# A two-layer hybrid diffusion trunk: modulation summed in halves of 512 features, rotated key and query rows put in place by GpSimd

## The chip, the cores and the metric

The kernel runs on one core of a Trainium2 chip. The metric is the device time of one execution in microseconds (us). A core has TensorE (PE, matmuls; its weight loads are listed as PEld), VectorE (DVE), ScalarE (ACT), GpSimd (POOL) and SyncE (SP), which issues nearly all transfers here. On-chip data lies in SBUF, results of PE in PSUM banks.

## What is computed

A trunk of two layers over 256 context and 256 latent tokens of 1024 features, in float32. Each layer modulates its normalised input by vectors made from a condition, runs three attention mixers on it, merges them by gates, and then runs a SwiGLU FFN. Cut to what matters:

```python
def adaln(cond, w, b):
    return jnp.split(jax.nn.silu(cond) @ w + b, 6, axis=-1)      # six kinds of 1024 features

for l in range(2):
    mx = adaln(c, w_ada[l], b_ada[l])                            # latent tokens
    mc = adaln(c_ctx, w_ada[l], b_ada[l])                        # context tokens
    hx = rms_norm(x, pre[l]) * (1 + mx[1]) + mx[0]               # hc alike, from ctx and mc
    kv = (rms_norm(ckv, kv_norm) @ w_ukv)                        # 8 heads: 64 of key, 64 of value
    q  = (rms_norm(cq, q_norm) @ w_uq)                           # 8 heads: 64 plain, 32 to be rotated
    qr, kr = rope_2d(q[..., 64:]), rope_2d(kr)                   # kr: one key of 32 for all heads
    scores = qn @ kn + qr @ kr                                   # 96 rows per head, then softmax
    ...                                                          # differential and windowed attention
    x = x + mx[2] * rms_norm(merge(o_a, o_b, o_c, gates), post[l])
    f = swiglu(rms_norm(x, ffn_pre[l]) * (1 + mx[4]) + mx[3])
    x = x + mx[5] * rms_norm(f, ffn_post[l])                     # context tokens alike in layer 0 only
```

Kinds 0, 1, 3 and 4 of the modulation scale and shift an input and are needed with features on partitions; kinds 2 and 5 (here called gates) multiply a sub-layer's output and are needed as rows that are the same on all partitions. The output is the latent stream after layer one.

## The kernel before

The token stream stands as four tiles of 128 tokens, two of context and two of latents; layer zero works on all four, layer one on the two latent tiles for queries and FFN. All weights come in blocks of up to 512 KB through SyncE into `raw` tiles (L166; three buffers) and are split into a high and a low part of a shorter float format: ACT casts the high part (L139, L142), DVE subtracts for the low one (L140, L143). A product is then three matmuls (`mm3`, L267 to L269: high by high, high by low, low by high).

PE and SyncE run what is issued to them in the order in which the program is written. For ACT, DVE and POOL a scheduler sets the order by priority, and code under `tc.high_priority()` goes ahead of what is ready at the same time.

`drive` (L241) writes that order: it runs the matmuls of the weight units one after another, counts their cost, and between them takes steps of an attention generator (`side`) and of a filler. The filler here is `ada_dve` (L341), the modulation's product. For each kind it goes through four quarters of 256 features. A quarter is two loads of 512 KB (`aw`, two buffers, L350); DVE multiplies each row by one element of the condition and accumulates, for the latent and the context condition apart (L401 the first piece, L403 the other seven of each): 16 pieces of 128x256 in all, or 8 where only one condition is needed. What is left is a sum over partitions, and that is `finish`, which is run half a quarter later: PE sums by matmuls with ones (L361), ACT copies the sums (L363), and for kinds 0, 1, 3 and 4 PE transposes them (L367) and DVE adds bias and weight (`mod_finish`). For a gate the sums go through DRAM: a row is written (L372), bias and norm weight are broadcast (L376, L377), the row is read back on all partitions (L380), and DVE adds and multiplies (L382, L383).

The filler serves layer zero's mixers (kinds 4, 3 and 2), layer zero's FFN (5 for layer zero; 1, 0, 4 and 3 for layer one), layer one's mixers (kind 2) and its FFN (kind 5): ten jobs of four quarters, 40 finishes, 24 with transposes, of which eight for one condition only (64 rows), and 16 for gates. In the FFN of layer zero PE meanwhile runs the gate and up projections; ACT applies the activation (L1271), DVE multiplies by the up part (L1272), and the product is split into `aT` by L139 and L140.

In the mixers `ukv` (L1025) makes keys and values of the latent attention for a group of four heads: two products for the keys, copied by ACT (L1033, L1034) into `kT` rows 0 to 63, four for the values, copied by DVE into `mv` (L1038), and four copies of the rotated shared key `krT` into rows 64 to 95 (L1040, DVE). `uq` (L1045) does the same for the queries: the rotated part goes through `rope` (L631: a shuffle and a multiply on DVE, a multiply and an add on POOL, L638 and L639) into a work tile, and four DVE copies put it into rows 64 to 95 of `qT` (L1061). The scores (L723), their maximum (L665), exponential (L669), scaling (L745, L747), combination of pairs (L805, L806), transposes (L675) and their copies (L678) are steps of the attention generator. L554 is the product for the first modulation vectors at the kernel's start, also with 32 columns of a condition and 256 columns of a weight.

## Time and profile before

| What | us |
|---|---|
| Median of three runs | 1523.82 |
| Lowest and highest of them | 1520.46 and 1524.37 |
| The profiled execution | 1522.53 |
| Its span in the trace | 1520.7 |
| PE busy in the span | 1457.6 |
| DVE busy in the span | 1022.9 |
| ACT busy in the span | 688.2 |
| POOL busy in the span | 154.6 |

PE is busy nearly all the time, so the profile is read from its gaps: first the table by stretches, which tells where they are, then the waits of PE, which tell what ended last in them, and then the timeline at the places named there. A wait in the lists of the other engines is of interest only where PE comes to wait behind it.

### The profile page before, as it was taken

How to read it: one execution, taken by the hardware profiler on the slowest of the kernel's cores; microseconds unless marked ns; L12 is line 12 of the kernel's file. 1: busy time of each engine (PE TensorE's matmuls, PEld its weight loads, DVE VectorE, ACT ScalarE, POOL GpSimd, SP SyncE). 2: the span in 40 equal slices, each digit the busy share in tenths (PEclk: the TensorE clock that was granted, in tenths of full speed). 3: DMA queues.
4: the chain of work that ended last, by engine and by line, in shares of the span. 5: the costliest groups of instructions: out<-in, count | busy, mean ns of one | idle time of the engine just before them, and what ended most of it. 6: DMA issues, size and time to landing. Idle time of an engine off the chain costs nothing. (4 is left out here: it accounts for less than half of the span.)

```text
span 1520.7 us, 23166 instructions
## 1 busy us (share of the span) xinstructions
PE 1457.6 (96%) x8827; PEld 1225.4 (81%) x8827; DVE 1022.9 (67%) x1987; ACT 688.2 (45%) x1293; POOL 154.6 (10%) x217
## 2 busy tenths in 40 slices
PE   7989999998999999999899999999999999999998
PEld 5867877776777879877676888877798899799986
DVE  4689768788884555778877314678667776666654
ACT  5566544444553354222222223666455564544443
POOL 1232100121100000000000000242102200100000
PEclk9999999999999999999999999999999999999999
DMA  9533222443333542665566225334345436567664
GB/s 290 154 108 98 66 88 85 110 111 111 98 97 101 172 144 73 184 182 171 180 206 198 95 97 170 108 80 139 94 116 142 132 100 195 180 209 218 207 213 166
DMA packets 254244, 216.25 MB, mean 142 GB/s; under 512 B 24427, under 2 KB 236085, under 8 KB 254133
## 3 DMA queue, kind: packets, MB, share of 16 engines
q1 hardware_dynamic: 252464, 209.98, 46.8%
q10 hardware_dynamic: 1668, 4.80, 0.8%
q8 instruction: 69, 1.13, 0.3%
q14 instruction: 43, 0.34, 0.1%
HBM read 209.48 MB, written 5.27 MB: 141 GB/s over the span
## 5 line engine op out<-in xcount | busy, mean ns | idle before, releaser
L267 PE MATMUL psg<-hT,hl 128*128 128x256 f32 (+1 forms) x1328 | 474.6, 357 | 0.0
L269 PE MATMUL psg<-hT,hl 128*128 128x256 f32 (+1 forms) x1328 | 449.4, 338 | 0.1
L268 PE MATMUL psg<-hT,hl 128*128 128x256 f32 (+1 forms) x1328 | 449.2, 338 | 0.3 <-DVE hT L460 0.3
L140 DVE TENSOR_TENSOR hl<-raw,hl 128x1024 fp32r<-128x1024 f32 (+2 forms) x243 | 291.1, 1199 | 207.2 <-ACT hl L139 206.4
L139 ACT CAST hl<-raw 128x1024 fp32r<-128x1024 f32 (+2 forms) x243 | 243.6, 1004 | 312.4 <-PE psg L269 176.7
L267 PEld LDWEIGHTS psg<-hT,hl 128*128 128x128 f32 x1328 | 252.9, 190 | 37.3 <-issue 13.9
L269 PEld LDWEIGHTS psg<-hT,hl 128*128 128x128 f32 x1328 | 252.4, 190 | 28.4 <-DVE hl L140 0.3
L268 PEld LDWEIGHTS psg<-hT,hl 128*128 128x128 f32 x1328 | 253.2, 191 | 24.6 <-issue 3.6
L403 DVE SCALAR_TENSOR_TENSOR acc<-aw,siluc,acc 128x256 f32<-128x256 f32 x448 | 200.2, 484 | 10.4 <-DMA aw<-in_w_ada 7.8
L477 POOL TENSOR_SCALAR smy<-ssy 128x1 f32<-128x1 f32 x12 | 4.1, 339 | 727.0 <-ACT work L298 727.0
L675 PE MATMUL psT<-ca,work 128*128 128x128 f32 x400 | 65.0, 277 | 10.4 <-DVE work L747 6.2
L669 ACT ACTIVATE work<-psS,nm 128x512 f32<-128x512 f32 (+1 forms) x96 | 59.1, 616 | 33.1 <-DVE nm L667 16.1
L267 PE MATMUL psg<-oT,hl 128*128 128x512 f32 (+1 forms) x192 | 69.5, 362 | 0.0
L675 PEld LDWEIGHTS psT<-ca,work 128*128 128x128 f32 x400 | 48.6, 142 | 22.6 <-issue 12.4
L665 DVE TENSOR_REDUCE nm<-psS 128x1 f32<-128x512 f32 (+1 forms) x96 | 57.1, 595 | 14.2 <-PE psS L723 8.9
L269 PE MATMUL psg<-oT,hl 128*128 128x512 f32 (+1 forms) x192 | 64.8, 338 | 0.2 <-DVE hl L140 0.2
L268 PE MATMUL psg<-oT,hl 128*128 128x512 f32 (+1 forms) x192 | 64.6, 337 | 0.0
L678 ACT COPY work<-psT 128x512 f32<-128x512 f32 (+1 forms) x72 | 36.8, 511 | 57.9 <-PE psT L675 56.5
L267 PE MATMUL psg<-hl,hT 128*128 128x256 f32 (+1 forms) x168 | 58.0, 345 | 1.9 <-ACT hT L139 1.9
L269 PE MATMUL psg<-hl,hT 128*128 128x256 f32 (+1 forms) x168 | 48.4, 288 | 0.6 <-DVE hT L140 0.6
L268 PE MATMUL psg<-hl,hT 128*128 128x256 f32 (+1 forms) x168 | 48.0, 286 | 0.0
L745 ACT ACTIVATE work<-work,rsd 128x512 f32<-128x512 f32 (+1 forms) x48 | 31.3, 652 | 36.2 <-DVE rsd L741 36.0
(324 smaller groups left out, 2578.5 us busy)
## 6 DMA issues: line engine op xcount, KB each, us to landing
raw<-in_w_gate_up SPq DMA_DIRECT2D x88, 512.0 KB
aw<-in_w_ada SPq DMA_DIRECT2D x80, 512.0 KB
raw<-in_w_in SPq DMA_DIRECT2D x78, 512.0 KB
raw<-in_w_down SPq DMA_DIRECT2D x44, 512.0 KB
aw<-in_w_ada SPq DMA_DIRECT2D x32, 256.0 KB
raw<-in_w_o SPq DMA_DIRECT2D x16, 512.0 KB
raw<-in_w_branch_a SPq DMA_DIRECT2D x8, 512.0 KB
raw<-in_w_in SPq DMA_DIRECT2D x16, 256.0 KB
```

The lines of the kernel that those rows point to most:

```text
L139: nc.scalar.copy(hi, src)
L140: nc.vector.tensor_tensor(lo, src, hi.bitcast(F32), ALU.subtract)
L267: nc.tensor.matmul(ps, lhsT=asl(a[0], k), rhs=bsl(b[0], k), start=st, stop=False)
L268: nc.tensor.matmul(ps, lhsT=asl(a[0], k), rhs=bsl(b[1], k), start=False, stop=False)
L269: nc.tensor.matmul(ps, lhsT=asl(a[1], k), rhs=bsl(b[0], k), start=False, stop=en)
L403: nc.vector.scalar_tensor_tensor(acc[:, s], w[:, k], sc, acc[:, s], ALU.mult, ALU.add)
L477: nc.gpsimd.tensor_scalar(sm, ss[:, 0:1], ss[:, 1:2], D * EPS, ALU.add, ALU.add)
L665: nc.vector.tensor_reduce(nm, ps[:, :nk], AX.X, ALU.max, negate=True)
L669: nc.scalar.activation(st["p"][:, :nk], ps[:, :nk], AF.Exp, bias=nm, accum_out=sm)
L675: nc.tensor.transpose(pt[:, k * P:(k + 1) * P], st["p"][:, k * P:(k + 1) * P], ident)
L678: nc.scalar.copy(st["pT"][:, :nk], pt[:, :nk])
L745: nc.scalar.activation(p, p, AF.Copy, scale=rs[:, j:j + 1])
```

## The change

Four things are changed. The modulation goes through halves of 512 features in place of quarters: four loads of two weight rows per partition instead of two loads of four, so 80 loads of 512 KB as before; accumulate pieces of 128x512, half as many; 20 finishes in place of 40, each with sums over 256 columns, one copy of 256 columns, two transposes in one PSUM bank, and for a gate rows of 512. The finish runs under high priority (`ahead_of`) after half of the next half's pieces, and it reports a higher cost to the filler's account. The filler of layer zero's mixers is started when 30 cost units of that stretch have passed, where before it was started ahead of it. And the copies of the rotated key into `kT` are made by POOL, issued at the start of `ukv`; in `uq` POOL adds the two rotated halves straight into the four head slices of `qT`, so that the work tile and DVE's four copies are gone.

```diff
@@ -228,6 +228,15 @@
                 return
             fill["acc"] -= v
 
+    def ahead_of(gen):
+
+        while True:
+            with tc.high_priority():
+                v = next(gen, None)
+            if v is None:
+                return
+            yield v
+
     def flush():
         if fill["D"] is not None:
             for _ in fill["D"]:
@@ -341,72 +350,78 @@
     def ada_dve(*jobs):
 
 
-        todo = [(l, kind, ns, q) for l, kind, ns in jobs for q in range(4)]
-
-        def raw(i, h):
-            l, kind, _, q = todo[i]
-            w = sp.tile([P, 4, 256], F32, tag="xt", bufs=2, name="aw")
-            c0 = kind * D + q * 256
-            nc.sync.dma_start(w, w_ada[l, h * 512:(h + 1) * 512, c0:c0 + 256].rearrange("(k p) n -> p k n", p=P))
+        H = D // 2
+        todo = [(l, kind, ns, hf) for l, kind, ns in jobs for hf in range(2)]
+
+        def raw(i, j):
+            l, kind, _, hf = todo[i]
+            w = sp.tile([P, 2, H], F32, tag="xt", bufs=2, name="aw")
+            c0 = kind * D + hf * H
+            nc.sync.dma_start(w, w_ada[l, j * 256:(j + 1) * 256, c0:c0 + H].rearrange("(k p) n -> p k n", p=P))
             return w
 
-        def finish(l, kind, ns, q, acc):
+        def finish(l, kind, ns, hf, acc):
             m = mods[l, kind]
             gate = kind in (2, 5)
             n = 64 * ns
             ps = bank("T")
-            for f in range(2):
+            for g in range(2):
                 for s in range(ns):
-                    j = 32 * (2 * s + f if gate else ns * f + s)
-                    nc.tensor.matmul(ps[j:j + 32, :P], lhsT=ones[:, :32], rhs=acc[:, s, f * P:(f + 1) * P], start=True, stop=True)
-            sums = work()[:, :P]
-            nc.scalar.copy(sums[:n], ps[:n, :P])
-            yield 0.8
+                    j = 32 * (2 * s + g if gate else ns * g + s)
+                    if gate:
+                        src = acc[:, s, g * 256:(g + 1) * 256]
+                    else:
+                        src = acc[:, s].rearrange("p (b g c) -> p b g c", b=2, g=2)[:, :, g]
+                    nc.tensor.matmul(ps[j:j + 32, :256], lhsT=ones[:, :32], rhs=src, start=True, stop=True)
+            sums = work()[:, :256]
+            nc.scalar.copy(sums[:n], ps[:n, :256])
+            yield 1.2
             if not gate:
                 ps = bank("T")
-                nc.tensor.transpose(ps[:, :n], sums[:n], ident[:n, :n])
-                mod_finish(l, kind, 2 * q, m, ps[:, :n].rearrange("p (f s z) -> p f s z", s=ns, z=32)[:, :, :, 0])
-                yield 0.2
+                for b in range(2):
+                    nc.tensor.transpose(ps[:, b * n:(b + 1) * n], sums[:n, b * P:(b + 1) * P], ident[:n, :n])
+                mod_finish(l, kind, 4 * hf, m, ps[:, :2 * n].rearrange("p (f s z) -> p f s z", s=ns, z=32)[:, :, :, 0])
+                yield 0.3
                 return
-            row = dp.tile([2 * ns, P], F32, name=f"row{l}_{kind}_{q}")
+            row = dp.tile([2 * ns, 256], F32, name=f"row{l}_{kind}_{hf}")
             nc.sync.dma_start(row, sums[0:n:32])
-            bw = work().rearrange("p (a b) -> p a b", a=2)
+            bw = [work(), work()]
             w = attn_post if kind == 2 else ffn_post
-            c0 = kind * D + q * 256
-            nc.sync.dma_start(bw[:, 0], b_ada[l:l + 1, c0:c0 + 256].to_broadcast([P, 256]))
-            nc.sync.dma_start(bw[:, 1], w[l:l + 1, q * 256:(q + 1) * 256].to_broadcast([P, 256]))
-            yield 1.0
-            mq = m[:, :ns, q * 256:(q + 1) * 256]
-            nc.sync.dma_start(mq, row.rearrange("(s f) p -> s (f p)", s=ns).rearrange("(o s) n -> o s n", o=1).to_broadcast([P, ns, 256]))
+            c0 = kind * D + hf * H
+            nc.sync.dma_start(bw[0], b_ada[l:l + 1, c0:c0 + H].to_broadcast([P, H]))
+            nc.sync.dma_start(bw[1], w[l:l + 1, hf * H:(hf + 1) * H].to_broadcast([P, H]))
+            yield 1.5
+            mq = m[:, :ns, hf * H:(hf + 1) * H]
+            nc.sync.dma_start(mq, row.rearrange("(s g) p -> s (g p)", s=ns).rearrange("(o s) n -> o s n", o=1).to_broadcast([P, ns, H]))
             for s in range(ns):
-                nc.vector.tensor_tensor(mq[:, s], mq[:, s], bw[:, 0], ALU.add)
-                nc.vector.scalar_tensor_tensor(mq[:, s], mq[:, s], 32.0, bw[:, 1], ALU.mult, ALU.mult)
-            yield 0.5 * ns
+                nc.vector.tensor_tensor(mq[:, s], mq[:, s], bw[0], ALU.add)
+                nc.vector.scalar_tensor_tensor(mq[:, s], mq[:, s], 32.0, bw[1], ALU.mult, ALU.mult)
+            yield 1.0 * ns
 
         nxt = raw(0, 0)
         pend = None
-        for i, (l, kind, ns, q) in enumerate(todo):
-            if q == 0:
+        for i, (l, kind, ns, hf) in enumerate(todo):
+            if hf == 0:
                 gate = kind in (2, 5)
                 mods[l, kind] = bp.tile([P, 2, D], F32, tag="gw", bufs=1, name="gw") if gate else mod_tile(kind)
-            acc = sp.tile([P, 2, 256], F32, tag="acc", bufs=2, name="acc")
-            for h in range(2):
+            acc = sp.tile([P, 2, H], F32, tag="acc", bufs=2, name="acc")
+            for j in range(4):
                 w = nxt
-                if h == 0 or i + 1 < len(todo):
-                    nxt = raw(i + h, 1 - h)
-                for k in range(4):
+                if j < 3 or i + 1 < len(todo):
+                    nxt = raw(i + j // 3, (j + 1) % 4)
+                for k in range(2):
                     for s in range(ns):
-                        sc = siluc[:, s, 4 * h + k:4 * h + k + 1]
-                        if h == 0 and k == 0:
+                        sc = siluc[:, s, 2 * j + k:2 * j + k + 1]
+                        if j == 0 and k == 0:
                             nc.vector.tensor_scalar(acc[:, s], w[:, k], sc, None, ALU.mult)
                         else:
                             nc.vector.scalar_tensor_tensor(acc[:, s], w[:, k], sc, acc[:, s], ALU.mult, ALU.add)
-                    yield 0.38 * ns
-                if h == 0 and pend is not None:
-                    yield from pend
-            pend = finish(l, kind, ns, q, acc)
+                    yield 0.76 * ns
+                if j == 1 and pend is not None:
+                    yield from ahead_of(pend)
+            pend = finish(l, kind, ns, hf, acc)
         yield 2.0
-        yield from pend
+        yield from ahead_of(pend)
 
 
     cur = {}
@@ -1027,6 +1042,8 @@
                 if g == 0:
                     env["mv"] = s8([P, 4, 512], F32, "mv")
                 kT = env["kT", g] = s8([P, 4, 512], F32, "kT")
+                for h in range(4):
+                    nc.gpsimd.tensor_copy(kT[64:96, h, :], env["krT"][64:96])
                 for h in range(0, 4, 2):
                     ps = bank()
                     yield from mm3(ps, parts, env["ckvT"], cols(h * 64, h * 64 + 128), full, range(2))
@@ -1036,8 +1053,6 @@
                     ps = bank()
                     yield from mm3(ps[:, :256], env["ckvT"], parts, tok(t), cols(256, 512), range(2))
                     nc.vector.tensor_copy(env["mv"][:, t, g * 256:(g + 1) * 256], ps[:, :256])
-                for h in range(4):
-                    nc.vector.tensor_copy(kT[64:96, h, :], env["krT"][64:96])
                 while put_off:
                     put_off.pop(0)()
             return f
@@ -1052,13 +1067,16 @@
                     nc.scalar.copy(qT[0:64, h + 1, TQ0:512], ps[64:128, :NQ])
                 ps = bank()
                 yield from mm3(ps[:, :NQ], parts, env["cqT"], cols(256, 384), cols(TQ0, 512), range(2))
-                r = work()
-                rope(r[:, :256], ps[:, NQ - 256:NQ], slice(0, P), c32, s32, SH8)
+                lat = ps[:, NQ - 256:NQ]
+                sh, t1 = (sp.tile([P, 256], F32, tag=tag, bufs=2, name=tag) for tag in ("rsh", "rt1"))
+                nc.vector.stream_shuffle(sh, lat, SH8)
+                nc.vector.tensor_tensor(t1, lat, c32, ALU.mult)
+                nc.gpsimd.tensor_tensor(sh, sh, s32, ALU.mult)
                 for h in range(4):
                     rows = slice(32 * h, 32 * h + 32)
                     if not last:
                         nc.scalar.copy(qT[64:96, h, 0:256], ps[rows, 0:256])
-                    nc.vector.tensor_copy(qT[64:96, h, 256:512], r[rows, :256])
+                    nc.gpsimd.tensor_tensor(qT[64:96, h, 256:512], t1[rows], sh[rows], ALU.add)
             return f
 
         for g in range(2):
@@ -1427,10 +1445,11 @@
                            lambda h, k: env["mv"][:, k, h * 64:(h + 1) * 64], False, lambda t: None)
         drive(1)
         if l == 0:
-            start_fill(ada_dve((0, 4, 2), (0, 3, 2), (0, 2, 2)), FR[0])
+            later = [(30.0, lambda: start_fill(ada_dve((0, 4, 2), (0, 3, 2), (0, 2, 2)), FR[0]))]
         else:
+            later = ()
             start_fill(ada_dve((1, 2, 1)), FR[2])
-        drive(count(("ukv", "uq", "dk", "dq", "dv")), attend(mla, PRM["LD"][0]), PRM["R1"][l])
+        drive(count(("ukv", "uq", "dk", "dq", "dv")), attend(mla, PRM["LD"][0]), PRM["R1"][l], later)
         drive(count(("gate", "branch", "s")) - 24, attend(diff_steps(l, env), PRM["LD"][1]), PRM["R2"][l])
         swa = head64_steps(l, env, "c", 2, lambda h, t, nk: stacked(env["sQ", h % 4 // 2][:, h % 2], env["sA"], env["sB"], h // 4, t, nk),
                            lambda h, k: env["sv"][:, k * P + 64 * (h // 4):k * P + 64 * (h // 4) + 64],
```

On ACT, in layer zero's gate and up projections, around the finish for whose copy PE waits in the trace of before. `hl` is a weight block's high part, `aT` the product of the FFN, `work<-psT` the copy of the sums, L1271 (L1289) the activation. Before:

```order
L139 CAST hl<-raw 128x1024
L1271 ACTIVATE work<-psg 128x512
L139 CAST hl<-raw 128x1024
L139 CAST aT<-work 128x512
L363 COPY work<-psT 128x128
L139 CAST hl<-raw 128x1024
```

And the finish at the same place after:

```order
L139 CAST hl<-raw 128x1024
L139 CAST aT<-work 128x512
L139 CAST hl<-raw 128x1024 x2
L377 COPY work<-psT 128x256
L1289 ACTIVATE work<-psg 128x512
L139 CAST aT<-work 128x512
```

The copy stood directly behind a cast of `aT`; now it stands behind two weight casts, and the activation and the next cast of `aT` follow it.

On DVE, in layer zero's mixers, from the first group's queries (`uq`) to the second group's values (`ukv`). `rt` and `rsh` are the two halves of the rotation, L143 is a weight split. Before:

```order
L636 STREAM_SHUFFLE rsh<-psg 128x256
L637 TENSOR_TENSOR rt_1130<-psg,cb 128x256
L143 SCALAR_TENSOR_TENSOR hl<-raw,hl 128x1024
L1061 COPY qT<-work 32x256 x4
L1038 COPY mv<-psg 128x256
L1040 COPY kT<-krT 32x512
```

After:

```order
L1072 STREAM_SHUFFLE rsh<-psg 128x256
L1073 TENSOR_TENSOR rt_1129<-psg,cb 128x256
L143 SCALAR_TENSOR_TENSOR hl<-raw,hl 128x1024
L1055 COPY mv<-psg 128x256 x4
L140 TENSOR_TENSOR hl<-raw,hl 128x1024
L680 TENSOR_REDUCE nm_1216<-psS 128x1 x2
```

The copies into `qT` between the weight split and the first `mv` copy are gone, and so is the `kT` copy that followed each of the four `mv` copies.

On POOL at the same place; the memset is that of the differential attention's keys. Before:

```order
L639 TENSOR_TENSOR work<-rt_985,rsh 128x256
L958 CAST dQA<-dQA 64x512 x2
L638 TENSOR_TENSOR rsh<-rsh,cb 128x256
L639 TENSOR_TENSOR work<-rt_1130,rsh 128x256
L963 MEMSET dB 64x512 x4
```

After:

```order
L973 CAST dQA<-dQA 64x512 x2
L1046 COPY kT<-krT 32x512 x4
L1074 TENSOR_TENSOR rsh<-rsh,cb 128x256
L1079 TENSOR_TENSOR qT<-rt_1129,rsh 32x256 x4
L978 MEMSET dB 64x512 x4
```

Four key copies have come in ahead of the rotation, and its one add has become four, which write `qT`.

## Rows read from the trace of the kernel before

**Rows 1.** Page, busy us of each engine (share of the span), instructions.
```profile
PE 1457.6 (96%) x8827; PEld 1225.4 (81%) x8827; DVE 1022.9 (67%) x1987; ACT 688.2 (45%) x1293; POOL 154.6 (10%) x217
```

**Rows 2.** Stretches of layer zero's FFN: us, PE, PEld, DVE, ACT, POOL, PEclk, DMA, GB/s.
```profile
600.00:850.00 250.00, 241.93 (x1153) 189.52 (x1153) 185.38 (x380) 69.50 (x103) 0.00 (x0) 0.99 0.60 181
850.00:960.00 110.00, 110.00 (x487) 91.09 (x486) 34.97 (x34) 31.80 (x43) 1.89 (x5) 1.00 0.35 116
```

**Rows 3.** Waits of PE: us in total, times, longest.
```profile
PE psS L723 <- ACT work L669: 7.5, 6, 3.2
PE psT L675 <- DVE work L747: 6.2, 6, 2.4
PE psT L367 <- ACT work L363: 5.9, 2, 5.3
PE psT L675 <- DVE work L806: 4.2, 6, 1.4
...
PE psT L361 <- DVE acc L403: 2.8, 2, 1.5
...
PE psg L267 <- DVE mv L1038: 2.1, 1, 2.1
```

**Rows 4.** Timeline, one visit of the sums: start us, us, engine, line, operation.
```profile
740.25 0.39 PE L268 MATMUL psg<-hT,hl 128*128 128x512 f32 x1
740.47 0.39 PE L269 MATMUL psg<-hT,hl 128*128 128x512 f32 x1
740.79 0.42 PE L361 MATMUL psT<-acc,ones 128*32 128x128 f32 x8
...
741.48 0.39 PE L268 MATMUL psg<-hT,hl 128*128 128x512 f32 x1
```

**Rows 5.** Timeline, one visit of a 64-row transpose, PE.
```profile
800.40 0.40 PE L269 MATMUL psg<-hT,hl 128*128 128x512 f32 x1
...
801.26 0.40 PE L268 MATMUL psg<-hT,hl 128*128 128x512 f32 x1
```

**Rows 6.** Instructions of single lines: ns min/median/max, first and last start.
```profile
L403 DVE SCALAR_TENSOR_TENSOR acc<-aw,siluc,acc x448: 458/478/1265, 111.0 to 1448.4; 128x256 f32<-128x256 f32 x150
...
L554 PE MATMUL psS<-aw,siluc x128: 379/379/644, 15.3 to 49.6; 128*32 128x256 f32 x128
...
L361 PE MATMUL psT<-acc,ones x256: 269/273/298, 146.3 to 1453.4; 128*32 128x128 f32 x128
```

**Rows 7.** Group by form, 512 features wide: busy us, mean ns, idle before.
```profile
L806 DVE SCALAR_TENSOR_TENSOR work<-work,rsd 128x512 f32<-128x512 f32 x16 | 12.0, 748 | 0.2
```

**Rows 8.** Timeline ahead of the long wait in the FFN.
```profile
724.54 0.62 DVE L401 TENSOR_SCALAR acc<-aw,siluc 128x256 f32<-128x256 f32 x2 [1.78 <-DMA aw<-in_w_ada]
...
727.45 0.68 DVE L1272 TENSOR_TENSOR work<-work,psg 128x512 f32<-128x512 f32 x1
...
728.69 0.26 ACT L363 COPY work<-psT 128x128 f32<-128x128 f32 x1
...
729.00 0.48 PE L367 MATMUL psT<-ca,work 128*128 128x128 f32 x1 [5.31 <-ACT work L363]
```

**Rows 9.** Stretches behind two waits of PE, columns as in rows 2.
```profile
100.40:103.60 3.20, 3.20 (x11) 2.72 (x11) 3.01 (x6) 1.04 (x1) 0.00 (x0) 0.50 0.00 0
728.50:731.80 3.30, 2.80 (x7) 2.26 (x8) 3.30 (x9) 0.44 (x2) 0.00 (x0) 0.50 0.35 85
```

**Rows 10.** Timeline, up-projections of layer zero.
```profile
94.62 1.58 POOL L639 TENSOR_TENSOR work<-rt,rsh 128x256 f32<-128x256 f32 x1
...
96.24 2.53 DVE L1061 COPY qT<-work 32x256 f32<-32x256 f32 x4 [0.61 <-POOL work L639]
...
99.28 0.38 PE L267 MATMUL psg<-hl,ckvT 128*128 128x256 f32 x1 [2.07 <-DVE mv L1038]
```

**Rows 11.** Timeline, the same line's add over 32 rows.
```profile
77.06 0.73 POOL L639 TENSOR_TENSOR krT<-rt,rsh 32x256 f32<-32x256 f32 x1
```

**Rows 12.** Waits of SyncE's queue: us in total, times, longest.
```profile
SPq L166 <- DVE acc L403: 68.1, 14, 9.2
```


## The prediction

> **What bounds the kernel now.** I read the engine totals first: TensorE (PE) is busy 1457.6 of 1520.7 us, the next engine, VectorE (DVE), 1022.9 [rows 1]. So time is won in two ways only: by less work on PE, and by shorter gaps in it. The table by stretches shows where the gaps are. In layer zero's FFN, while its gate and up projections run and the modulation is a filler between their weight blocks, PE works 241.93 of 250 us; in the down projection behind it, where there is no filler, 110.00 of 110 [rows 2]. The waits of PE then say what ended last in the gaps. Three kinds matter: the scores and probabilities of attention (L723, L675), the modulation's own two steps on PE (its sums L361, its transpose L367), and one wait for `mv`, the copied values of the up-projection [rows 3]. The profiled execution took 1522.53 us, 1.8 above its span; the median of the runs is 1.3 above that. I make the sum on the span and add both. About 0.3% is what a measurement of this kernel can tell from no change: faster is below 1519.2, slower above 1528.4.
>
> **Halves instead of quarters, on PE.** Per finish PE leaves its stream of FFN matmuls for the sums. Two of these start 0.22 apart; around the sums the distance is 741.48 - 740.47 = 1.01, in place of two such pitches, so a visit costs 1.01 - 0.44 = 0.57 [rows 4]. There are 40 visits, 22.8 in all, and 20 after. A visit has as many matmuls as before, each over 256 columns in place of 128. The kernel has rows for both widths: 379 ns for 256 columns (L554), 273 for 128 (L361) [rows 6], so 0.106 more. A visit has two groups behind one another, so I add 0.21: 20 x 0.78 = 15.6, and 7.2 are saved. The transposes behind the sums are as many as before, in half as many visits. For layer one's kinds they have 64 rows, and there a visit costs 801.26 - 800.40 - 0.44 = 0.42 [rows 5]; eight such become four with two transposes, the second at about a quarter: 8 x 0.42 - 4 x 0.53 = 1.3. I take nothing for the 128-row ones. All of this lies on the path, as PE is full around it. **-8.5**; were the wider columns to cost twice the rows' difference, -4.3.
>
> **What PE waits for in the finishes.** 5.9 us are spent in front of the transpose L367, 5.3 of them in one wait [rows 3]. The timeline tells how it came about. DVE has its first accumulate held by a load until 724.54, then has eight pieces in line, and the FFN's multiply (L1272) comes only behind them at 727.45. ScalarE (ACT) has the cast of that product (`aT`) next in its order, and the sums' copy (L363) behind it. It is done at 728.69 + 0.26, and PE goes on at 729.00 [rows 8]. In the changed order this copy stands in front of the next activation and two weight casts behind the cast of the product before, and PE has nine matmuls between sums and transpose, not six. So the wait has no longer a cause at this place: what is late next there is a weight cast, which PE needs anyway. Of the ten such copies in the FFN three stand directly behind an `aT` cast, ten of twenty did before, with one long stall among them; one left is worth 5.3 and its clock below. The sums L361 waited 2.8 for the accumulator [rows 3]. They are issued eight pieces behind it, as before, but a piece is now twice as wide, so that about twice the work of DVE lies between. **-8.7** for both. Behind the long stop the granted clock is 0.50, the lower of PE's two levels (1.2 GHz), for 3.3 us [rows 9]; without it half of this is won, **-1.7**.
>
> **DVE.** A piece over 256 features takes 478 ns [rows 6], one of the same kind over 512 took 748 in the attention's combination [rows 7]. With the first pieces alike, 512 x 0.478 = 245 us become 256 x 0.748 = 191: about 50 us fewer on an engine that is not the bound, by itself worth nothing. It counts where attention's steps wait in DVE's line, below. As the first loads of layer zero are 30 cost units later, the first accumulates come later too; the gate's finishes fall into the projections of the last branch, with PE work enough behind them before the gate is used.
>
> **The rotated rows.** Before, GpSimd (POOL) adds the two rotated halves at 94.62 for 1.58, then DVE copies four head slices from 96.24 for 2.53, and the four copies of `mv` stand behind these, each followed by a key copy. PE waits 2.07 for the first `mv` and starts at 99.28 [rows 10]; behind it the clock is 0.50 for 3.2 us [rows 9]. In the changed order the four `mv` copies follow the weight split directly; no POOL result stands in front of them. **-2.1 and -1.6.** POOL writes the four slices itself: an add of 32 rows by 256 took 0.73 with no other engine in its way [rows 11], so four take 2.9 to (at 1.58 each) 6.3, from 94.62 to between 97.5 and 100.9. DVE's copies ended at 98.77, and the scores that read the slices stand behind the `mv` matmuls, later than 99.28. The key copies (32 by 512) are twice as wide: 4 x 0.73 to 4 x 1.46, issued ahead of the whole up-projection, which covers them.
>
> The Trainium skill ("SBUF — State Buffer", section "Who interferes with whom") says that DVE and GpSimd share a pair of ports, and that an instruction that loses the race for it is blocked for the whole of the other's. The two durations of that add above (0.73 and 1.58) would fit it; what it makes of the time here is the third rival.
>
> **Attention's waits.** L723 for the exponential, L675 for the scaled probabilities (L747) and for the combination (L806) come to 7.5 + 6.2 + 4.2 = 17.9 [rows 3]. All of them have DVE in their chain, with modulation pieces in its line. Fewer, longer pieces cut both ways: half as many stand ahead, but one that has just begun lasts 0.27 longer [rows 6, 7], and 18 such waits, each longer by that, are +4.9. I take **-3**, between -9 (half of all goes) and +5.
>
> **New costs.** The finish now goes ahead of other work on ACT and DVE (a sums copy of twice the width, gate multiplies of 512), and POOL's longer adds hold whatever reads `qT` first. No row prices this directly; 20 finishes at the 0.26 of the copy [rows 8] are 5.2, and two waits like the one for `mv` [rows 10] 4.1, so up to +9, down to 0. Nearly all of it is off the path: **+2**.
>
> **Sum.** -8.5 - 8.7 - 1.7 - 2.1 - 1.6 - 3 + 2 = -23.6. The span becomes 1497.1, the execution 1498.9, and the median 1500.2. With the unknown terms at their ends: attention -9 and no new cost 1492.2; attention +5 and new costs +9 1515.2.
>
> **Rivals.**
> - Only PE's work goes (-8.5); the waits come back at other places, as ACT's order is new everywhere and a wait of that size needs one late load: 1515.3. For it: of twenty finishes in that FFN one had a long stall, which is as much chance as order. If just one such stall stays (5.3 + 1.7), 1507.2.
> - More goes than I take. With half as many pieces on DVE, attention's waits fall by 9 and with them two or three more stretches of lower clock, at 1.6 each as in [rows 9]: about 1488.
> - GpSimd becomes the bound of the up-projection. There are four such places (two groups, two layers). If POOL's four adds all go at 1.58 and DVE is held by them, 6.3 replaces 1.58 + 2.53, 2.2 more for the scores; the `mv` wait of 2.1 stays and each place falls to the lower clock for 1.6: 5.9 x 4 = 23.6, and all that was gained is gone: 1523.8. Against it: the scores stand well behind, and three of the four places have no such wait now.
> - Slower: SyncE's queue. It runs in written order, and already a weight load stood behind an accumulate for up to 9.2 us, 68.1 in 14 waits [rows 12]. A load buffer is now held by pieces of twice the width, four loads per finish in one run, so that a weight block may come too late for PE. Each stall like that at 729 costs 5.3 + 1.7 = 7.0; from the fourth the gain is gone, and with five it is 23.6 - 35 = -11.4, a median of 1535. Against it: the loads have the same size and number, and a buffer is held by less DVE time than before.
>
> **Chances.** The forecast 0.58 (own range 1492 to 1515), only PE's work 0.15, more goes 0.09, GpSimd 0.09, SyncE's queue 0.09. So faster 0.82, no difference 0.09, slower 0.09. The range leaves out the last two: 1488 to 1518.
>
> **What would show it.** Right: the sums' group with 20 visits of about 0.78; 224 + 32 accumulates at about 0.75; no wait of PE for the sums' copy or the accumulator in the FFN; no stretch at clock 0.50 near 100 and near 728; no wait for `mv`; PE above 98% in the gate and up projections of layer zero's FFN. Wrong: a new row of PE waiting for POOL's `qT`, POOL adds at 1.58 throughout with DVE idle beside them, accumulates well above 0.75, or PE waiting for weight parts with SyncE's load behind an accumulate.

## The result, and the profile of the changed kernel

The changed kernel takes 1498.34 us (median of four runs, 1496.77 to 1501.83); the kernel before, run beside it, 1523.8. The ratio is 0.9837, with a 95% interval from 0.9823 to 0.9852. Forecast were 1500.2, in a range from 1488 to 1518. The profiled execution took 1499.38; its span is 1497.3, where the sum had said 1497.1. The sum came out closer than its parts, as is told below.

Engine totals of the changed kernel, the answer to [rows 1]: busy us, share of the span, instructions.

```profile
PE 1445.3 (97%) x8699; PEld 1223.0 (82%) x8699; DVE 974.4 (65%) x1657; ACT 687.6 (46%) x1273; POOL 176.1 (12%) x245
```

PE's busy time fell by 12.3 us, DVE's by 48.5. The rest of the 23.4 us came out of gaps in PE's work. The lower clock is no part of it: by the granted clock of the two traces both executions spent some 21 us at 0.50 behind the first 40 us, at other places. The stretch of layer zero's gate and up projections, the answer to [rows 2] (us, PE, PEld, DVE, ACT, POOL, PEclk, DMA, GB/s):

```profile
592.00:842.00 250.00, 250.00 (x1156) 200.76 (x1155) 169.89 (x237) 72.16 (x97) 0.00 (x0) 1.00 0.60 187
```

PE is busy for all of it, at the full clock; before, it was 241.93 of 250. The waits of PE, the answer to [rows 3] (us in total, times, longest):

```profile
PE psS L738 <- ACT work L684: 8.8, 5, 5.8
PE psT L690 <- DVE work L762: 5.7, 4, 2.8
...
PE psT L382 <- ACT work L377: 3.0, 1, 3.0
...
PE psg L276 <- ACT qT L1078: 1.6, 1, 1.6
...
PE psT L690 <- DVE work L821: 1.4, 4, 0.5
```

The waits for the accumulator and for `mv` have no row any more; the one for the sums' copy is 3.0 in place of 5.9, but at another place. The lead of the changed kernel by stage can be read off PE: both kernels have 2208 records of the first of the three matmuls (L267, now L276) in the same order, so the same one can be looked up in both traces:

| First matmul, number | Place | Before, us | After, us | Lead |
|---|---|---|---|---|
| 72 | ahead of the up-projections | 65.1 | 65.0 | 0.2 |
| 120 | behind them | 106.3 | 101.9 | 4.4 |
| 360 | layer zero's mixers | 340.0 | 329.3 | 10.7 |
| 576 | its output projection | 541.0 | 534.9 | 6.1 |
| 600 | ahead of its FFN | 560.8 | 552.2 | 8.6 |
| 1008 | end of the gate and up projections | 847.2 | 822.8 | 24.4 |
| 1584 | layer one, windowed attention | 1215.2 | 1192.3 | 22.9 |
| end | span | 1520.7 | 1497.3 | 23.4 |

Two thirds come from layer zero's FFN, 4 us from the up-projections, another 4 from the mixers between them, and layer one gives 1 back.

### The profile page after: what moved, and what is told of

It is laid out like the page before. It is cut to its first block, busy times and chain, and to the rows that moved or that the text cites. A ratio compares the mean times of both kernels' runs of the same rounds, so it can differ in the third digit from the quotient of the medians.

```text
span 1497.3 us, 22535 instructions
## 1 busy us (share of the span) xinstructions
PE 1445.3 (97%) x8699; PEld 1223.0 (82%) x8699; DVE 974.4 (65%) x1657; ACT 687.6 (46%) x1273; POOL 176.1 (12%) x245
## 5 line engine op out<-in xcount | busy, mean ns | idle before, releaser
L276 PE MATMUL psg<-hT,hl 128*128 128x256 f32 (+1 forms) x1328 | 472.3, 356 | 0.0
L276 PEld LDWEIGHTS psg<-hT,hl 128*128 128x128 f32 x1328 | 253.2, 191 | 37.7 <-issue 14.8
L418 DVE SCALAR_TENSOR_TENSOR acc<-aw,siluc,acc 128x512 f32<-128x512 f32 x224 | 161.6, 749 | 28.4 <-DMA aw<-in_w_ada 27.0
L680 DVE TENSOR_REDUCE nm<-psS 128x1 f32<-128x512 f32 (+1 forms) x96 | 57.2, 598 | 31.1 <-PE psS L738 22.9
L276 PE MATMUL psg<-oT,hl 128*128 128x512 f32 (+1 forms) x192 | 69.0, 360 | 0.0
L276 PE MATMUL psg<-hl,hT 128*128 128x256 f32 (+1 forms) x168 | 57.5, 342 | 1.6 <-ACT hT L139 1.6
L738 PE MATMUL psS<-kT,qT 96*128 96x512 f32 (+1 forms) x96 | 43.2, 532 | 2.1 <-ACT work L684 2.1
```

Of the source, the lines that this page charges most:

```text
L276: nc.tensor.matmul(ps, lhsT=asl(a[0], k), rhs=bsl(b[0], k), start=st, stop=False)
L418: nc.vector.scalar_tensor_tensor(acc[:, s], w[:, k], sc, acc[:, s], ALU.mult, ALU.add)
L680: nc.vector.tensor_reduce(nm, ps[:, :nk], AX.X, ALU.max, negate=True)
L738: nc.tensor.matmul(st["ps"][:, :nk], lhsT=q, rhs=k, start=z == 0, stop=z == len(ops) - 1 and mk is None)
```

## The experiments

Spans below are of one traced execution each; ratios are those of the times, against the kernel before. The executions of one kernel spread over 2 to 10 us, in span as in time (the four of the changed kernel have spans from 1495.0 to 1499.0), so a difference of a few us between two spans is told from chance only by the ratio beside it, or by the place in the trace at which it arises.

**The rows' part alone.** The kernel before with GpSimd's key copies and its adds into `qT`:

```diff
                 kT = env["kT", g] = s8([P, 4, 512], F32, "kT")
+                for h in range(4):
+                    nc.gpsimd.tensor_copy(kT[64:96, h, :], env["krT"][64:96])
...
-                for h in range(4):
-                    nc.vector.tensor_copy(kT[64:96, h, :], env["krT"][64:96])
                 while put_off:
...
-                rope(r[:, :256], ps[:, NQ - 256:NQ], slice(0, P), c32, s32, SH8)
...
-                    nc.vector.tensor_copy(qT[64:96, h, 256:512], r[rows, :256])
+                    nc.gpsimd.tensor_tensor(qT[64:96, h, 256:512], t1[rows], sh[rows], ALU.add)
```

> The kernel before with one part of the change alone: GpSimd makes the key copies and adds the rotated query halves straight into qT; the modulation stays in quarters and starts where it did. My theory: the wait for mv near 99 (2.1) and the low clock behind it (1.6) go, so the lead over the kernel before is 3.7 to 4.3 us by the end of the up-projections (at 106 the changed kernel leads by 4.45) and stays: about 1519.5. Rival (GpSimd bounds the up-projections): the add into qT is waited for by the scores, a new row of PE waiting for GpSimd, and the time is within 1 us of before or above it.

Measured: 0.9968 (0.9953 to 0.9983), span 1517.5, so 3.2 less (4.9 by the ratio); no row of PE waiting for GpSimd. The rival falls; of the theory the wait for `mv` went, but a stretch at the lower clock stayed. By the up-projections' end the lead was 2.7, not 4.4 as in the changed kernel, and the reason is the clock. The stretch from 96 to 103 in this kernel, and then in the changed one:

```profile
96.00:103.00 7.00, 6.13 (x28) 5.41 (x28) 3.50 (x8) 2.94 (x5) 4.78 (x8) 0.76 0.42 117
```

```profile
96.00:103.00 7.00, 5.87 (x36) 4.93 (x34) 4.12 (x10) 4.41 (x11) 4.59 (x8) 1.00 0.59 149
```

Ahead of it both have the same wait of PE at the same matmul, 1.61 us for ACT's copies into `qT`; behind it the granted clock was 0.50 for some 3.4 us in the one execution (a mean of 0.76 over 7 us) and full in the other.

**The modulation's part alone.** The changed kernel with that diff taken back:

> The changed kernel with the rotated rows made as before (DVE copies for keys and queries, one GpSimd add): the modulation's part alone. My theory: the two parts lie at different places and add, so this one is about 4 us behind the changed kernel: 1502.5, with the wait for mv back near 96. Rival: the freed DVE time of the rows' part also pays elsewhere, then this one is 6 us or more behind, 1504.5 and above.

Measured: 0.9881 (0.9862 to 0.9899), span 1501.6: 4.3 behind the changed kernel, 19.1 ahead of the one before. By spans 3.2 + 19.1 = 22.3 of 23.4, by the ratios 0.32% + 1.19% = 1.51% of 1.63%: the parts add, within the intervals. The wait for `mv` is back, 2.06 us, but not the lower clock behind it, which the kernel before has in the same stretch [rows 9]:

```profile
100.40:103.60 3.20, 3.08 (x17) 2.36 (x16) 3.08 (x6) 1.13 (x2) 0.00 (x0) 1.00 0.00 0
```

The median of 1504.29 lies between the two expectations and does not decide.

**Which half of the rows' part.** First the queries' adds alone, then the key copies alone, in the kernel before:

> The kernel before with GpSimd's adds into qT alone; the key copies stay on DVE. The rows' part as a whole gave 3.2 us of span (1520.7 to 1517.5). My theory: DVE's four copies of 2.53 held the first mv, so this half takes away the wait near 99 and the low clock behind it, and little else: a span of about 1518.5, with the gaps of the first group's values (0.76, 0.43 and 0.39 near 81 to 84) still there. Rival: the key copies between the mv copies hold PE as well, then the wait near 99 shrinks but stays above 1 us.

> The kernel before with the key copies alone on GpSimd, at the start of ukv; the queries' copies stay on DVE. My theory: it gives the 1.4 us of the first group (the lead of the rows' part up to 84) and leaves the wait for mv near 99 at 2 us, because the first mv copy stands behind the queries' copies: a span of about 1519.3. Rival: it takes the wait near 99 away, then 1517.5 and the queries' adds are worth nothing.

Measured: queries 0.9979 (0.9965 to 0.9993), span 1518.2; keys 0.9995 (0.9983 to 1.0007), span 1522.0. With the queries' adds the wait for `mv` shrinks from 2.1 to 0.7, no lower clock follows, and the first group's gaps stay. With the key copies alone the wait is there and longer. Waits of PE, queries and then keys:

```profile
PE psg L267 <- DVE mv L1038: 0.7, 1, 0.7
```

```profile
PE psg L267 <- DVE mv L1040: 2.8, 1, 2.8
```

With the keys alone the theory held for the first group, which gains the 1.5 expected, but not for the total: the second group loses 2.8, as PE comes earlier to it, waits 1.6 for the copies into `qT` and 2.8 for the `mv` copy that stands behind them in DVE's order, and the clock is 0.50 for 6.8 us from 98.3 on, twice as long as before. By time the key copies alone can't be told from no change. The queries' adds carry the part; what the keys add to them, 0.7 by spans, is not clear of the spread.

**Halves, finished in quarters.** The changed kernel with 40 finishes, each with the widths of the kernel before:

```diff
-            pend = finish(l, kind, ns, hf, acc)
+            pend = [finish(l, kind, ns, 2 * hf + z, acc[:, :, z * 256:(z + 1) * 256]) for z in range(2)]
...
-                if j == 1 and pend is not None:
-                    yield from ahead_of(pend)
+                if j in (1, 3) and pend is not None:
+                    yield from ahead_of(pend[j // 2])
```

> The changed kernel, accumulating over 512 features, but finished in quarters: 40 visits of the sums with 128 columns, 24 transposes in visits of one, gate rows of 256. My theory of the size of PE's term: 7.2 + 1.3 = 8.5 us come back, 1506.8. In its ACT order 9 of the 20 copies of sums in layer zero's FFN stand directly behind a cast of aT, as 10 of 20 did before and 3 of 10 after the change. If that order is what made the wait of 5.3 near 729, waits of PE for the copy come back too, 3 us or more in the FFN: 1510 or above. Rival: the wait came from DVE's many short pieces, and with wide ones it stays away: 1506.8 and no such row above 1 us in the FFN.

Measured: 0.9925 (0.9903 to 0.9947), span 1509.3, 12.0 behind the changed kernel. In the FFN all that PE waited for a sums' copy is this:

```profile
PE psT L377 <- ACT work L373: 1.0, 1, 1.0
```

So the order of copies behind `aT` casts is not enough for the long wait, and on that the rival was right; the time that it gave with this, 1506.8, was 4.4 too low (median 1511.16). In that FFN the kernel loses 6.5 us on the changed one (by the same matmuls as in the table above): 1.2 by this gap, which leaves 5.3 for PE's own work, where the sum had 20 x 0.57 - 10 x 0.78 + 1.3 = 4.9. Of the other 5.5 most lies at three places: 1.5 by the lower clock behind the gap at 97, 1.9 around the start of the FFN, 1.7 at the flush of the last finish.

**Another rate.** The kernel before with one number changed:

```diff
-"FR": (0.42, 0.642, 0.21, 0.134),
+"FR": (0.42, 0.66, 0.21, 0.134),
```

> The kernel before with one number changed: the filler's rate in layer zero's FFN 0.66 in place of 0.642. Work and tile sizes stay; the finishes come about 3% sooner among the FFN's matmuls, and 4 of 20 copies of sums stand behind a cast of aT in ACT's order, not 10. My theory: the wait of 5.3 near 729 is a meeting of a late load and that order, so it goes (below 1.5) with the lower clock behind it, 5 to 7 us: a span of 1514 to 1516. Rival: short pieces make such a wait wherever the finish stands: PE waits 4 us or more for a sums' copy somewhere in that FFN again, and the span is 1519 or above.

Measured: 0.9929 (0.9912 to 0.9945), span 1512.2, so 8.5 less (10.8 by the ratio), without anything of the change; 7.6 of the 8.5 arise in that FFN, by the matmuls of the table. The theory holds, with somewhat more than the 5 to 7 expected, and the rival falls: quarters, with their short pieces, do without the stall. By its trace 5 of the 20 copies stand behind an `aT` cast, not 4. Waits of PE for the modulation:

```profile
PE psT L361 <- DVE acc L403: 2.1, 2, 1.2
...
PE psT L367 <- ACT work L363: 0.6, 1, 0.6
```

Of L367's wait for the copy of sums 0.6 is left, of 5.9. So the stall of 5.3 was a meeting, and the traces show what met. In the kernel before DVE stood 5.02 for a modulation load, then took twelve pieces in one run; SyncE meanwhile could not issue the next weight block, whose buffer waited for DVE's split, until 718.73, and only behind it came the modulation load that DVE had until 724.54 [rows 8]:

```profile
712.99 0.61 DVE L401 TENSOR_SCALAR acc<-aw,siluc 128x256 f32<-128x256 f32 x2 [5.02 <-DMA aw<-in_w_ada]
...
718.73 0.37 SPq L166 DMA_DIRECT2D raw<-in_w_gate_up  x1
719.15 0.58 SPq L350 DMA_DIRECT2D aw<-in_w_ada  x1
```

With the other rate no such load is so late; the longest that DVE waits for one in that FFN behind 660 us is this:

```profile
718.73 2.47 DVE L403 SCALAR_TENSOR_TENSOR acc<-aw,siluc,acc 128x256 f32<-128x256 f32 x6 [1.52 <-DMA aw<-in_w_ada]
```

The five kernels that have the stall (the one before, the rows' part, queries, keys, the later quarters) all have that first wait too, 3.8 to 5.3 us. The one with halves finished in quarters has neither, although 9 of its copies stand behind a cast. The size of the stall moves with where the rest of the kernel stands. Queries alone, keys alone:

```profile
PE psT L367 <- ACT work L363: 6.1, 2, 5.5
```

```profile
PE psT L367 <- ACT work L363: 3.8, 2, 3.2
```

**The later start.** The changed kernel with the filler started at once, and then the kernel before with the filler started later:

```diff
-            later = [(30.0, lambda: start_fill(ada_dve((0, 4, 2), (0, 3, 2), (0, 2, 2)), FR[0]))]
+            later = [(0.0, lambda: start_fill(ada_dve((0, 4, 2), (0, 3, 2), (0, 2, 2)), FR[0]))]
```

> The changed kernel with the filler of layer zero's mixers started at the first cost unit of that stretch, not the thirtieth. The prediction gave the later start no price. My theory: it is worth little by itself and only moves the finishes: the wait of 3.0 for the sums' copy near 341, which stands behind a cast that waits for GpSimd's rotation, goes, and accumulates come between the up-projections and the first softmax steps: within 2 us of the changed kernel, a span of 1495.5 to 1499.5. Rival: the later start is what made attention's waits fall between 106 and 340 (the changed kernel gains about 6 us there); then 1501 or above.

> The kernel before with the filler of layer zero's mixers started 30 cost units later, all else as before. The changed kernel lost 6.2 us of span when this part was taken out. My theory: the later start keeps accumulates out of the up-projections and of the first softmax steps whatever their width, so it gives some 3 us here too: a span of about 1517.5. Rival: the 6.2 us were where the finishes happened to come among attention's steps; then there is no gain here, 1520 or above, with other waits of L723 and L675 in place of those of before.

Measured: the changed kernel without it 0.9881 (0.9856 to 0.9906), span 1503.5, so 6.2 more; the kernel before with it 1.0039 (1.0026 to 1.0051), span 1524.8, so 4.1 more. Waits of PE in the two:

```profile
PE psS L738 <- ACT work L684: 11.9, 5, 5.4
PE psT L690 <- DVE work L762: 6.6, 3, 2.6
...
PE psT L690 <- DVE work L821: 4.1, 4, 2.8
```

```profile
PE psS L723 <- ACT work L669: 13.0, 5, 6.9
PE psT L675 <- DVE work L806: 6.1, 5, 4.7
...
PE psT L675 <- DVE work L747: 5.2, 3, 2.1
PE psT L367 <- ACT work L363: 4.8, 1, 4.8
```

In each it is attention's waits that grew, from 15.9 and 17.9 in sum to 22.6 and 24.3. My theory missed both; the rivals hold: the later start shows no value of its own, it decides where the finishes and accumulates meet attention's steps, and by spans it is worth 6 us in one kernel and costs 4 in the other (by the ratios 6.7 and 5.9).

**The gate's multiplies.** In the changed kernel PE's longest wait is near 1181. DVE had the gate's multiply in its line ahead of the windowed attention's maxima, and the row that it needs was issued late by SyncE. Timeline (start us, us, engine, line, operation, idle before and what ended it):

```profile
1172.53 0.50 SPq L395 DMA_DIRECT2D gw<-row  x1
...
1177.36 0.69 DVE L397 TENSOR_TENSOR gw<-gw,work 128x512 f32<-128x512 f32 x1 [3.25 <-DMA gw<-row]
...
1180.90 1.22 PE L738 MATMUL psS<-sk,sQ 128*128 128x512 f32 x2 [5.81 <-ACT work L684]
```

Two kernels put a pause ahead of these multiplies, first everywhere (without the condition), then, as here, in layer one's mixers only:

```diff
+            if l and kind == 2:
+                yield 3.0
             for s in range(ns):
                 nc.vector.tensor_tensor(mq[:, s], mq[:, s], bw[0], ALU.add)
```

> The changed kernel with one pause more (3 cost units) between the gate row's read and DVE's multiplies on it. In the changed kernel DVE stands 3.25 us at the first of these multiplies near 1177 while the row is under way; behind it stand the first maxima of the windowed attention, and PE waits 5.81 for what follows them, with the clock at 0.50 behind. My theory: that wait falls to about the 3.2 it was before, with less of the lower clock: 3 to 4 us, about 1495. Rival: the next thing in DVE's line is late anyway (the maxima, a weight split), and it is within 1 us of the changed kernel, 1498.

> The changed kernel with the pause ahead of the gate's multiplies in layer one's mixers only. The pause everywhere took the wait of 5.81 near 1181 down to 3.2, but it slowed the filler so that the last finish of layer one's FFN was flushed right behind its accumulates, with a new wait of PE of 7.7. My theory: with the pause in one job the new wait is gone and 1.6 to 2.6 us are left: a span of about 1495.3. Rival: the flush at the end of layer one's mixers takes the place of that in the FFN, a wait of PE for the accumulator there, and 1497.3 or above.

Measured: everywhere 0.9905 (0.9889 to 0.9922), span 1506.4, which neither theory had; in one job 0.9823 (0.9798 to 0.9848), span 1494.8. The pause everywhere took the wait near 1181 away and made a longer one at the end of layer one's FFN, as the filler was not done when its stretch ended and its rest was flushed at once:

```profile
1435.61 1.54 DVE L419 SCALAR_TENSOR_TENSOR acc<-aw,siluc,acc 128x512 f32<-128x512 f32 x2 [3.13 <-DMA aw<-in_w_ada]
...
1437.20 1.07 PE L375 MATMUL psT<-acc,ones 128*32 128x256 f32 x4 [7.67 <-DVE acc L419]
```

In the second kernel that is gone, and what is left of the wait is what the kernel before had:

```profile
PE psS L740 <- ACT work L686: 6.1, 5, 3.2
```

By span it is 2.5 below the changed kernel, by the ratio 2.1, though this execution too had the lower clock behind the gap near 96. On this one, the start at 45 cost units:

> The kernel with the pause in layer one's mixers (a span of 1494.8), its filler in layer zero's mixers started at 45 cost units in place of 30. My theory: the start moves finishes among attention's steps, and where they meet is chance: the wait of 3.0 near 341 moves or goes, another comes: 1491 to 1499. If later is better by itself, 1492 or below; if the gate's row then comes too late for the norm behind the mixers, a wait of DVE for the row and PE behind it near 535, 1498 or above.

Measured: 0.9815 (0.98 to 0.983), span 1494.2: the places of the waits moved (5.5 the longest of L740, no wait for the sums' copy), the sum did not. Both kernels are the fastest of this document by their traces; by times their intervals overlap with that of the changed kernel.

**The priority.** The changed kernel with the finishes at normal priority (and the same for the last one):

```diff
-                    yield from ahead_of(pend)
+                    yield from pend
```

> The changed kernel with the finishes at normal priority. In the order of all five engines it has no instruction in another place than the changed kernel. My theory: the priority does nothing, the same time, a span within 1 us of 1497.3 and PE's waits at the same places. Rival: none that the order allows; the difference of the two shows what two executions of the same program can differ by.

Measured: 0.9834 (0.9819 to 0.9849), span 1498.3. The expectation has the order wrong. It is the same on PE, GpSimd and SyncE, but by the two traces two copies of sums on ACT, and the small steps of four finishes on DVE, stand one or a few places later without the priority. Near 341 the copy comes behind both casts of `sQ`, where with the priority it came between them (shown below), and PE waits 3.71, not 2.99:

```profile
340.24 1.26 ACT L985 CAST sQ<-work 64x512 fp32r<-64x512 f32 x2 [4.98 <-POOL work L654]
...
341.52 0.37 ACT L377 COPY work<-psT 128x256 f32<-128x256 f32 x1
...
341.94 0.69 PE L382 MATMUL psT<-ca,work 128*128 128x128 f32 x2 [3.71 <-ACT work L377]
```

So the priority does move finishes ahead, but in time it can't be told from nothing (0.9834 and 0.9837). Nor is the 1.0 between the two spans a measure of what two executions of one program differ by. At matmul 576 this execution was 3.9 behind that of the changed kernel: 0.5 from the start on, 0.7 by this wait, and most of the rest by the lower clock, which lasted 6.8 us longer between matmuls 360 and 576. The changed kernel's own lead of 6.1 at that matmul is to be read with that in mind.

## Why the prediction was right, and where it was not

**PE's work in the finishes (-8.5): right.** The visit after, the answer to [rows 4] (start us, us):

```profile
708.16 0.39 PE L278 MATMUL psg<-hT,hl 128*128 128x512 f32 x1
708.48 0.64 PE L375 MATMUL psT<-acc,ones 128*32 128x256 f32 x8
709.05 0.50 PE L276 MATMUL psg<-hT,hl 128*128 128x512 f32 x1
709.39 0.39 PE L277 MATMUL psg<-hT,hl 128*128 128x512 f32 x1
```

709.39 - 708.16 - 0.44 = 0.79, where 0.78 was worked out from the two widths in [rows 6]. Read the same way, all ten visits in this FFN cost 0.77 to 0.79, and 0.56 or 0.57 in the kernel before wherever nothing was waited for. Two transposes of 64 rows cost 0.48 or 0.49 in a visit, where 0.53 was taken; so eight visits become four for 1.4 (the prediction's own 8 x 0.42 - 4 x 0.53 is 1.2, not 1.3). For the FFN this makes 5.0, the sum had 4.9, and the run with 40 finishes leaves 5.3. The pieces and the sums by line, the answer to [rows 6] (ns min/median/max):

```profile
L418 DVE SCALAR_TENSOR_TENSOR acc<-aw,siluc,acc x224: 728/746/1223, 166.5 to 1420.7; 128x512 f32<-128x512 f32 x112
...
L375 PE MATMUL psT<-acc,ones x128: 379/391/403, 239.7 to 1429.7; 128*32 128x256 f32 x128
```

The 512-wide piece has a median of 746, as the row from the attention had said; DVE lost 48.5 us, forecast about 50.

**The FFN's waits (-8.7 and -1.7): the size was right, the reason only in part.** The lead grew by 15.8 in this stretch; 8.7 + 1.7 and 4.9 of PE's work are 15.3. The steps of the stall were as the timeline had shown. But I put its end down to the new place of the copy in ACT's order, and counted three of ten copies behind an `aT` cast where the changed kernel's trace has four. With halves finished in quarters 9 of 20 copies stood behind one, and there was no such wait; with another rate there was none in quarters either. What both have in common with the changed kernel is that no modulation load is so late there: the changed kernel's DVE waits at most 2.13 for one behind 610 us, where it had waited 5.02. One execution, that without the priority, has a load waited for 3.76 and another 2.32, and no stall of PE, so halves may bear a late load better; that is one trace, and why a load is late in one kernel and not in another was not tested. Of the lower clock, -1.7 was fairly taken: in all five kernels with the stall the clock fell with it. The rival that called the stall chance was right on its cause. That waits come back at other places, its second half, came true in the mixers (3.0 for the sums' copy, below) and not in this FFN.

**The up-projections (-3.7): the sum right, the terms not.** The wait for `mv` is gone, but another was right behind it. Timeline of the changed kernel, the answer to [rows 10]:

```profile
94.03 1.73 DVE L143 SCALAR_TENSOR_TENSOR hl<-raw,hl 128x1024 fp32r<-128x1024 f32 x1
...
94.77 4.03 POOL L1079 TENSOR_TENSOR qT<-rt,rsh 32x256 f32<-32x256 f32 x4
...
95.68 0.39 PE L276 MATMUL psg<-hl,ckvT 128*128 128x256 f32 x1 [1.61 <-ACT qT L1078]
95.69 0.41 DVE L1055 COPY mv<-psg 128x256 f32<-128x256 f32 x1
```

The first of the four adds alone, and then, of the kernel before, PE's start at the same matmul:

```profile
94.77 1.60 POOL L1079 TENSOR_TENSOR qT<-rt,rsh 32x256 f32<-32x256 f32 x1
```

```profile
96.23 0.39 PE L267 MATMUL psg<-hl,ckvT 128*128 128x256 f32 x1 [0.53 <-ACT qT L1060]
```

PE now waits 1.61 for ACT's copies into `qT`, where it had waited 0.53 for them; so the second group gained 1.2 in gaps and 1.6 by the clock, in this execution. The clock's part was no safe term: behind the same wait of 2.1 for `mv` the clock fell in the kernel before and with the other rate, and stayed full in the modulation's part alone and with the later quarters. The first group gave 1.4 more, which I had not priced: the key copies had held `mv` there too, by three gaps below 0.8 each. GpSimd's four adds took 4.03 us, between the 2.9 and the 6.3 given, and no engine waited for them: that rival fell. The first took 1.60, the others some 0.8; the first ran beside a weight split of DVE, which lasted from 94.03 to 95.76, and ended 0.60 behind it. In the kernel before 18 adds of L639 took 1.49 or more, and every one of them ended 0.58 to 0.60 behind a weight split of DVE with two inputs in SBUF. The Trainium skill ("SBUF — State Buffer", section "Who interferes with whom") has it that the loser of the ports that DVE and GpSimd share is held for the whole of the other's instruction; by that the traces agree, since 0.6 is not much below the 0.73 that such an add takes by itself [rows 11].

**Attention's waits (-3): right in the sum only.** They went from 17.9 to 8.8 + 5.7 + 1.4 = 15.9. The moves are larger: the lead grew by 6.3 between matmuls 120 and 360 and fell by 4.6 up to 576. The prediction gave the later start nothing; it moved these waits by -6.7 in one kernel and by +6.4 in the other, so my bounds of -9 and +5 were of the right size, and the -3 between them had no ground: that it came out near is luck. (The rival with attention at -9 and two or three lower clocks fewer comes to 1489 to 1491 by its own terms, not 1488.)

**New costs (+2): too small.** Two waits came that had a mechanism I had not named. Near 341 the copy of the sums stands on ACT behind a cast that waits for GpSimd's rotation:

```profile
339.78 0.62 ACT L985 CAST sQ<-work 64x512 fp32r<-64x512 f32 x1 [4.98 <-POOL work L654]
340.31 0.36 ACT L377 COPY work<-psT 128x256 f32<-128x256 f32 x1
...
340.72 0.69 PE L382 MATMUL psT<-ca,work 128*128 128x128 f32 x2 [2.99 <-ACT work L377]
```

It cost 3.0, and 1.5 by the lower clock behind it (0.57 over 3.5 us):

```profile
340.50:344.00 3.50, 3.28 (x10) 2.73 (x11) 2.22 (x6) 2.03 (x4) 0.34 (x1) 0.57 0.51 141
```

The other is the gate's multiply ahead of the maxima, 5.81 against 3.16 before. Together about 7, with a second stretch at the lower clock behind the latter, of 6.8 us in place of 3.4, not counted. I had looked at the gate in layer zero, where PE has work behind it, and not in layer one.

**The rival on SyncE's queue fell.** Its weight loads stood 2.8 us in all behind an accumulate, where it had been 68.1 behind L403 [rows 12] and 35.3 behind L401:

```profile
SPq L166 <- DVE acc L416: 2.8, 1, 2.8
```

**Not foreseen at all** is a gain of 2.5 at the output projection (matmuls 576 to 600): before, PE waited there for DVE, which had a weight split in hand whose block had landed late:

```profile
547.71 1.05 ACT L139 CAST kept<-raw 128x1024 fp32r<-128x1024 f32 x1 [4.11 <-DMA raw<-in_w_gate_up]
...
548.79 1.23 DVE L140 TENSOR_TENSOR kept<-raw,kept 128x1024 fp32r<-128x1024 f32 x1 [3.94 <-ACT kept L139]
...
550.67 0.50 PE L267 MATMUL psg<-kept,mh 128*128 128x512 f32 x1 [1.32 <-DVE work L475]
```

PE's waits in that stretch were this one and one of 0.71, and after the change there is none; no run isolates it. With 1.4 in the first group and the good side of attention in layer zero it paid for the new waits.

## What to carry to other kernels

Work taken off the engine that bounds the kernel can be priced from a few rows of the trace: 0.78 a visit was worked out, 0.77 to 0.79 measured, and it held wherever the rest moved. A wait that is a meeting of a late load with an order of instructions can go with any change that shifts one of them, so before a rewrite is given the credit, one number that shifts the same work (here the filler's rate, 8.5 of the 23.4 us) should be tried; against that kernel the changed one leads by 14.9. A copy that is moved off an engine gains only down to the next thing that PE waits for at that place, and a result that comes by DMA should not stand in an engine's line ahead of a step that PE needs.

## What the runs showed of the hardware

The same wait of PE, 1.61 or 1.62 us at the same matmul of the up-projections, stands in nine of these traces. In one of them, with the key copies alone, a second wait follows six matmuls later. Of the other eight, in three the granted clock fell from 2.4 to 1.2 GHz behind it for 3.4 us, which cost 1.5; in five it stayed. The kernel with the pause in layer one alone is among the three, the changed kernel among the five, and up to there the order of the two is the same on every engine. The wait of 2.1 for `mv` a little later stands in four traces, and behind it the clock fell in two. The Trainium skill ("TensorE: Matmul & The Clock Gate", section "Part 1: The HAM clock gate") says that the gate's look at activity is not tied to the kernel's start, so that the point of a change varies from run to run; these traces fit that, and here not only the point varied but whether the clock fell at all. For a sum it means that a lower clock behind a gap of this size is a chance, not a term.

In the kernel before, 18 of the 30 adds of GpSimd over 128x256 (L639) took 1.49 to 1.79 us in place of 0.73, all of them begun while DVE had a weight split in hand. So the price of such an add hangs here on what DVE does at its start, and the same add can cost twice as much at another place.
